# A two-layer decoder trunk on one core: the projection chunk with the sparse attention's keys and compressed input is put ahead of the chunk with its queries

## The chip, the cores and the metric

The kernel runs on one core of a Trainium2 chip. Its five instruction streams are TensorE (PE, with its weight loads as PEld), VectorE (DVE), ScalarE (ACT), GpSimd (POOL) and SyncE (SP, which here only issues DMAs). The metric is the time of one execution on the device, in microseconds (us).

## The reference

`x` is 256 tokens of 1024 numbers in float32. Each of two layers does this:

```python
x = x + 0.5 * swiglu_ffn(x, ffn1_norm[l], ffn1_wi[l], ffn1_wo[l])
h = rms_norm(x, mix_norm[l])
(sb_q, sb_k, sb_v, mla_cq, mla_ckv, mla_kr, nsa_q, ck, cv, sk, sv, wk, wv,
 nsa_gate, merge_gate) = jnp.split(h @ w_in[l], offsets, axis=-1)
o_sb  = stick_breaking_attention(sb_q, sb_k, sb_v)        # 8 heads of 64
o_mla = mla_attention(mla_cq, mla_ckv, mla_kr, ...)       # 8 heads, low rank
o_nsa = nsa_attention(nsa_q, ck, cv, sk, sv, wk, wv, nsa_gate, ...)
gates = jax.nn.sigmoid(merge_gate)
y = gates[0] * (o_sb @ proj_sb[l]) + gates[1] * (o_mla @ proj_mla[l]) \
  + gates[2] * (o_nsa @ proj_nsa[l])
x = x + y @ w_out[l]
x = x + 0.5 * swiglu_ffn(x, ffn2_norm[l], ffn2_wi[l], ffn2_wo[l])
```

In the sparse attention (NSA), `ck` and `cv` are the compressed input: windows of 32 tokens, 16 apart, get a position added and go through a two-layer network, which makes 15 compressed keys and values for each of two groups. `sk`, `wk` are the keys of its other two branches and `nsa_q` its queries; these are normalized and rotated.

## The kernel before, in words

The 256 tokens lie as two blocks `t` of 128. Every float32 operand is split into a high and a low half, and each product is three matmuls (`mm3`, L588 to L590: high by high, low by high, high by low, in the order in which the trace names them).

The mixer between the two feed-forward nets multiplies the normalized `h` with the input projection in chunks of 512 or fewer columns. The weights come in slabs of 256 rows. A slab is loaded on SP's queue, either as float32 (`raw`, L514, then split by ACT in L1042 and DVE in L1044) or from a copy that an earlier part of the program split already (`early`, L1030: four DMAs, two `whi` and two `wlo`). Four slab buffers go round. `t_chunk` (L1080) takes slab after slab: for each it issues 12 matmuls of 512 columns, six for each token block; a chunk of 1024 rows is 4 slabs and 48 matmuls. After a block's last matmul it starts the block's evacuation.

Which slab comes when is the list that `layer_plan` writes, and which chunk uses it is the order of the calls in `bulk()`; both have to agree. The two chunks of this case are

- the queries' chunk, columns 1952 to 2463 of `w_in`. Its evacuation `ev_nq` (L1393) is one ACT copy for each block into `nx` (L1395);
- the keys' chunk, 512 columns picked from 2464 on. Its evacuation `ev_nk` (L1398) copies the compressed input `ck`, `cv` into a scratch buffer `c2` (L1404, ACT), sends it by two SP DMAs for each block into the tile `zc`, in which two neighbouring tokens share a partition (L1406), and copies the keys into `nx` (L1412).

`zc` is read by `cmp_in` (L1804): four PE transposes (L1809) that wait for all four DMAs, DVE additions of the position (L1821), and a split into `zw` (L1068 on ACT, L1070 on DVE). `zw` is used much later, by the compression network. `nsa_prep` (L1761) normalizes and rotates queries and keys of a block together, so it needs both evacuations.

Beside `bulk()` other tasks of the mixer run: stick-breaking attention (`sb_head`, scores L1552 and L1558, ACT and DVE work on them, the reversal L1585 and L1586 on PE, `pv` with PV matmuls L1522 to L1528), and MLA, whose queries and keys are turned on DVE (`turn`, L1247), written to DRAM by POOL (L1249, `md`) and read back by POOL (L1257, `st`) in a layout for the scores. POOL also raises sums to a power for the norms (L595). MLA's softmax ends on ACT (L1668), and PE transposes its result (L1677).

All these tasks are generators. A `Planner` holds a clock for each of PE, ACT, DVE and POOL, with costs written in the program, asks each task for its next step, and gives the engine to the step that could start first, with small handicaps (`HOLDS`, `URGENCY`). The instructions of PE, DVE and ACT are written in the order of its choice. The queues of SP and POOL have their DMAs in the order in which the planner came to them, and an instruction that waits holds up those behind it. In the planner's clock a zc DMA lands 4.2 us after its copy:

```python
            z = Tok(k2.t + 4.2)
            s_wf.put(z)
            ev_zc[t].set(z)
```

Nothing measured goes back into it: the order is fixed when the program is built.

Of the kernel before, what the change touches and what calls it, by code (L numbers as in the profile page):

```python
# [16 lines left out]
D = 1024  # L17
# [5 lines left out]
KT = D // 128  # L23
# [9 lines left out]
def _k_slabs(rows, n, get, name="_fn"):  # L33

    kts = rows // 128
    g = min(kts, max(1, 1024 // n))
    out = []
    for k0 in range(0, kts, g):
        gg = min(g, kts - k0)

        def fn(inp, l, k0=k0, gg=gg):
            w = np.asarray(get(inp, l))[k0 * 128:(k0 + gg) * 128]
            return w.reshape(gg, 128, n).transpose(1, 0, 2).reshape(128, gg * n)

        fn.__name__ = name
        out.append((gg * n, fn))
    return out


def _cols(name, c0, n):  # L50
    return lambda inp, l: inp[name][l][:, c0:c0 + n]


def _cat(name, parts):
    return lambda inp, l: np.concatenate([np.asarray(inp[name][l][:, a:a + n]) for a, n in parts], 1)
# [7 lines left out]
def _w1(name, j0):  # L63
    def w1_slab(inp, l):
        w = np.asarray(inp[name][l]).reshape(16, 128, 128)[j0:j0 + 8]
        return w.transpose(1, 0, 2).reshape(128, 1024)
    return w1_slab


def layer_plan():  # L70

    plan = []

    def ffn(p):
        f0, fn = FFN_CHUNKS[0]
        plan.extend(_k_slabs(D, 2 * fn, _cat(p + "_wi", [(f0, fn), (DFF + f0, fn)])))
        for f0, fn in FFN_CHUNKS[1:]:
            for part in range(2):
                plan.extend(_k_slabs(D, fn, _cols(p + "_wi", part * DFF + f0, fn)))
        for kt in range(DFF // 128):  # L80
            plan.append((1024, lambda inp, l, kt=kt: inp[p + "_wo"][l][kt * 128:(kt + 1) * 128]))

    def merge(b, name):
        out = []
        for c in range(2):
            out.extend(_k_slabs(D, 512, _cols("w_in", 3256 + b * 1024 + c * 512, 512)))
            out.extend(_k_slabs(512, 512, _cols(name, c * 512, 512)))
        return out

    ffn("ffn1")  # L90
    plan.extend(_k_slabs(D, 440, _cat("w_in", [(1536, 416), (3232, 24)])))
    plan.extend(_k_slabs(D, 512, _cols("w_in", 0, 512)))
    plan.extend(_k_slabs(256, 768, lambda inp, l: inp["mla_w_uq"][l], "_uq"))
    sk = _k_slabs(D, 512, _cols("w_in", 512, 512))
    plan.extend(sk[:2])
    plan.append((1024, _ukv))
    plan.extend(sk[2:])
    plan.extend(_k_slabs(D, 512, _cols("w_in", 1024, 512)))
    plan.extend(_k_slabs(D, 512, _cols("w_in", 1952, 512)))
    plan.extend(_k_slabs(D, 512, _cat("w_in", [(2464, 128), (2592, 128), (2720, 128), (2976, 128)])))  # L100
    m = merge(0, "proj_sb")
    plan.extend(m[:4])
    plan.extend(_k_slabs(D, 256, _cat("w_in", [(2848, 128), (3104, 128)])))
    m = m[4:] + merge(1, "proj_mla")
    plan.extend(m[:W1K_AT])
    plan.extend((1024, _w1("cmp_wk1", j0)) for j0 in (0, 8))
    plan.extend(m[W1K_AT:W1V_AT])
    plan.extend((1024, _w1("cmp_wv1", j0)) for j0 in (0, 8))
    plan.extend(m[W1V_AT:])
    m = merge(2, "proj_nsa")  # L110
    plan.extend(m[0:4] + m[6:10] + m[4:6] + m[10:])
    for kt in range(KT):
        plan.append((1024, lambda inp, l, kt=kt: inp["w_out"][l][kt * 128:(kt + 1) * 128]))
    ffn("ffn2")
    return plan
# [127 lines left out]
class Planner:  # L243
# [11 lines left out]
    def spawn(self, gen, hold=0.0):  # L255
        try:
            self.live.append([hold, gen, next(gen)])
        except StopIteration:
            pass
# [68 lines left out]
def use_p(cols, count, *deps, slots=(), extra=0.0):  # L328

    o = count * max(cols / 2400.0 + 0.0135, 0.06) + extra  # L330
    return "P", o, o + 0.2, deps, slots
# [40 lines left out]
def decoder_trunk(ctx, tc, xt_in, wts, lcon, cst, out, depth=DEPTH):  # L372
    nc = tc.nc
    PSUM = bass.MemoryType.PSUM
    plan = layer_plan()
# [9 lines left out]
    def acc_tile():  # L385
        return pb.tile([128, 512], F, tag="ps", name="acc")
# [12 lines left out]
    def cut(pair, *ix):  # L399
        return pair[0][ix], pair[1][ix]  # L400
# [96 lines left out]
    def slab_at(i):  # L497
        l, j = stream[i]
        return l * LSZ + offs[j], plan[j][0], plan[j][1].__name__
# [86 lines left out]
    def mm3(o, a, b, start=False, stop=False, **kw):  # L586

        nc.tensor.matmul(o, a[0], b[0], start=start, stop=False, **kw)  # L588
        nc.tensor.matmul(o, a[0], b[1], start=False, stop=False, **kw)  # L589
        nc.tensor.matmul(o, a[1], b[0], start=False, stop=stop, **kw)  # L590
# [13 lines left out]
    def of_t(q):  # L604
        return [(q[0][:, :, t, :], q[1][:, :, t, :]) for t in range(NT)]
# [342 lines left out]
    def mixer(l):  # L948
        es = ExitStack()
        mp = es.enter_context(tc.tile_pool(name="mp", bufs=1))  # L950
        hT, sq = nxt[0]
        nxt_T = hT
        hT = of_t(hT)
# [55 lines left out]
        def take():  # L1009
            use_at[0] += 1  # L1010
            return use_at[0] - 1

        def mark():
            ev_used[used[0]].set(Tok(pl.clock["P"]))
            used[0] += 1
# [58 lines left out]
        def t_chunk(n, kts, lhs, evac, need=lambda t, k: ()):  # L1074
            g = min(kts, max(1, 1024 // n))
            ns = kts // g
            acc = [None] * NT
            for s in range(ns):
                while slab_at(use_at[0])[2] in side:
                    yield from side[slab_at(use_at[0])[2]]()  # L1080
                i = take()
                for t in range(NT):
                    for j in range(g):
                        k = s * g + j
                        e = slab_ev[i][0 if (j + 1) * n <= RAW else 1]
                        tok = yield use_p(n, 3, e, *need(t, k), slots=(s_acc,) if k == 0 else ())
                        if k == 0:
                            acc[t] = acc_tile()
                        sl = slabs[i][1]
                        mm3(acc[t][:, :n], cut(lhs[t], A, k, A), cut(sl, A, slice(j * n, (j + 1) * n)),  # L1090
                            start=k == 0, stop=k == kts - 1)
                    if s == ns - 1:
                        spawn(evac(t, acc[t], tok), 0.02)
                s_w.put(tok)
                mark()
# [68 lines left out]
        def lat():  # L1164

            js = [take() for _ in range(4)]
            a = [None] * NT
            for k in range(KT):
                i = js[k // 2]
                for t in range(NT):  # L1170
                    tok = yield use_p(440, 3, slab_ev[i][k % 2], ev_hT[k], slots=() if k else (s_acc,))
                    if not k:
                        a[t] = acc_tile()
                    mm3(a[t][:, :440], cut(hT[t], A, k, A), cut(slabs[i][1], A, slice((k % 2) * 440, (k % 2 + 1) * 440)),
                        start=k == 0, stop=k == KT - 1)
                    if k == KT - 1:
                        spawn(ev_lat(t, a[t], tok), 0.02)
                if k % 2:
                    s_w.put(tok)
                    mark()  # L1180
# [287 lines left out]
        def bulk():  # L1468
            yield from lat()
            yield from chunk_T(sb_qk(0, 0.125))  # L1470
            for t in range(NT):
                nc.sync.dma_start(xd[t], xs[t])
            yield from chunk_T(sb_qk(1, 1.0))
            yield from t_chunk(512, KT, hT, ev_v)
            yield from t_chunk(512, KT, hT, ev_nq)
            yield from t_chunk(512, KT, hT, ev_nk)
            yield from t_chunk(512, KT, hT, ev_gate_raw)
            yield from t_chunk(256, KT, hT, ev_rest)
            yield from merge(0, g0, ev_g0, o_sb, ev_osb, True)
            for b, (oT, ev_o) in enumerate(((o_sb, ev_osb), (o_mla, ev_omla))):  # L1480
                for c in range(2):
                    if b or c:
                        ths, ev = [None] * NT, events(NT)
                        yield from t_chunk(512, KT, hT, gate_ev(ths, ev))
                        yield from merge(c, ths, ev, oT, ev_o, b == 0)
                if b == 0:
                    ev_sbm.set(Tok(pl.clock["P"]))
            gs = [([None] * NT, events(NT)) for _ in range(2)]
            for c in range(2):
                yield from t_chunk(512, KT, hT, gate_ev(*gs[c]))  # L1490
            for c in range(2):
                yield from merge(c, *gs[c], o_nsa, ev_onsa, False, final=True)
# [715 lines left out]
```

## Time and profile before

| | us |
|---|---|
| median of 3 runs (lowest, highest) | 1247.59 (1246.65, 1249.44) |
| the profiled execution | 1247.43 |
| its span, first to last instruction | 1245.5 |
| PE busy in it | 1238.7 |
| DVE busy | 944.4 |
| ACT busy | 789.4 |
| POOL busy | 153.6 |
| granted PE clock | 1.000 |

How to read the lines: PE is TensorE's matmuls, PEld its weight loads, which overlap them. `L1809` is a line of the kernel, `tp<-ident,zc` the tiles written and read. A row of a timeline gives the start in us, the length, the engine, the line and the operation, its form, how many in a row (`x4`), and in brackets how long the engine stood idle before and what released it. Matmul lengths overlap one another, so the distance from start to start is what a matmul costs. `SPq` is SP's queue: the length there is that of the issue (or of a wait before the next), not of the transfer. Rows that end with `KB` and a number are DMA issues of a window: how many, the size of one, and the median us from issue to landing.

The queries' chunk ended near 252 us in layer 0 and 871 us in layer 1 (the first rows of L1395 at 252.33 and 871.30), the keys' chunk near 266 and 888 us (L1404 ran from 266.2 to 888.9).

### The profile page before, as it was taken

What the parts mean: (1) busy time and instruction counts of PE and PEld (TensorE: products, weight loads), DVE (VectorE), ACT (ScalarE), POOL (GpSimd) and SP (SyncE); (2) the same over time, 40 slices, a digit from 0 to 9 for tenths busy, and PEclk for the clock granted to TensorE, in tenths of its full rate; (3) what the DMA queues carried; (4) which work ended last, traced back from release to release, by engine and by line L of the source; (5) the groups of instructions that cost most, each with busy time, mean ns of one, the idle gap of its engine ahead of it and who ended that gap; (6) DMA issues with size and microseconds to landing.
All of it is one profiled execution on the core that took longest, in us unless ns stands there. A gap on an engine that the chain in (4) does not pass through costs nothing.

```text
span 1245.5 us, 26170 instructions
## 1 busy us (share of the span) xinstructions
PE 1238.7 (99%) x9318; PEld 1159.4 (93%) x9318; DVE 944.4 (76%) x1961; ACT 789.4 (63%) x1633; POOL 153.6 (12%) x247
## 2 busy tenths in 40 slices
PE   9999999999999999999999999999999999999998
PEld 9999999888878899999999999998888889999987
DVE  7876668988888777776578776689968987786644
ACT  6665557787887566565456565567767774565542
POOL 0011201232000001121001121013330000023000
PEclk9999999999999999999999999999999999999999
DMA  8899985677645568999768999666897555667653
GB/s 273 287 329 326 339 269 184 197 209 234 217 128 171 166 214 260 332 331 337 215 202 279 331 321 321 221 203 188 286 317 240 157 156 185 192 209 245 220 169 119
DMA packets 157122, 298.20 MB, mean 239 GB/s; under 512 B 21424, under 2 KB 24496, under 8 KB 156992
## 3 DMA queue, kind: packets, MB, share of 16 engines
q1 hardware_dynamic: 143872, 258.64, 64.9%
q0 software_dynamic: 13120, 37.89, 8.2%
q8 instruction: 73, 1.20, 0.4%
q14 instruction: 57, 0.47, 0.1%
HBM read 258.12 MB, written 37.81 MB: 238 GB/s over the span
## 4 chain that ended last, share of the span: by engine, by line
PE 94%; ACT 2%; DVE 2%; DMA 1%; issue 1%; POOL 0%; SPq 0%; DVEq 0%; ACTq 0%; POOLq 0%
PE acc L780 13%; PE acc L778 13%; PE acc L779 13%; PE acc L588 9%; PE acc L590 9%; PE acc L589 9%; PE acc L670 6%; PE acc L669 6%; PE acc L668 6%; PE acc L1204 1%; PE acc L1205 1%; PE acc L1206 1%; PE att L2041 1%; ACT wf L1636 1%; PE tp L2052 1%
## 5 line engine op out<-in xcount | busy, mean ns | idle before, releaser
L536 DVE TENSOR_TENSOR vlo<-raw,vhi 128x512 fp32r<-128x512 f32 x452 | 292.7, 685 | 90.9 <-ACT vhi L535 89.4
L535 ACT ACTIVATE vhi<-raw 128x512 fp32r<-128x512 f32 x452 | 263.5, 622 | 142.8 <-PE acc L779 43.1
L778 PE MATMUL acc<-hThi,vhi 128*128 128x256 f32 x1280 | 353.3, 276 | 0.0
L779 PE MATMUL acc<-hTlo,vhi 128*128 128x256 f32 x1280 | 353.3, 276 | 0.0
L780 PE MATMUL acc<-hThi,vlo 128*128 128x256 f32 x1280 | 353.3, 276 | 0.0
L780 PEld LDWEIGHTS acc<-hThi,vlo 128*128 128x128 f32 x1280 | 240.3, 188 | 0.0
L779 PEld LDWEIGHTS acc<-hTlo,vhi 128*128 128x128 f32 x1280 | 240.3, 188 | 0.0
L778 PEld LDWEIGHTS acc<-hThi,vhi 128*128 128x128 f32 x1280 | 240.3, 188 | 0.0
L1044 DVE TENSOR_TENSOR wlo<-raw,whi 128x512 fp32r<-128x512 f32 x216 | 141.2, 679 | 30.4 <-ACT whi L1042 28.6
L1042 ACT ACTIVATE whi<-raw 128x512 fp32r<-128x512 f32 x216 | 124.9, 616 | 47.8 <-PE acc L590 17.8
L670 PE MATMUL acc<-gh,vlo 128*128 128x256 f32 x528 | 145.7, 276 | 0.0
L668 PE MATMUL acc<-gh,vhi 128*128 128x256 f32 x528 | 145.7, 276 | 0.0
L669 PE MATMUL acc<-gl,vhi 128*128 128x256 f32 x528 | 145.7, 276 | 0.0
L588 PE MATMUL acc<-whi,hThi 128*128 128x512 f32 (+2 forms) x352 | 138.1, 392 | 0.0
L590 PE MATMUL acc<-whi,hTlo 128*128 128x512 f32 (+2 forms) x352 | 133.4, 379 | 0.0
L589 PE MATMUL acc<-wlo,hThi 128*128 128x512 f32 (+2 forms) x352 | 133.4, 379 | 0.0
L536 DVE TENSOR_TENSOR wlo<-raw,whi 128x512 fp32r<-128x512 f32 (+2 forms) x109 | 69.9, 677 | 45.4 <-ACT whi L535 45.1
L535 ACT ACTIVATE whi<-raw 128x512 fp32r<-128x512 f32 (+2 forms) x109 | 63.2, 617 | 57.7 <-PE acc L590 26.4
L554 ACT ACTIVATE ehi<-eraw 128x512 fp32r<-128x512 f32 x60 | 38.0, 633 | 97.3 <-DMA eraw<-in_wts 95.7
L669 PEld LDWEIGHTS acc<-gl,vhi 128*128 128x128 f32 x528 | 99.1, 188 | 0.0
L670 PEld LDWEIGHTS acc<-gh,vlo 128*128 128x128 f32 x528 | 99.1, 188 | 0.0
L668 PEld LDWEIGHTS acc<-gh,vhi 128*128 128x128 f32 x528 | 99.1, 188 | 0.0
(350 smaller groups left out, 2502.1 us busy)
## 6 DMA issues: line engine op xcount, KB each, us to landing
raw<-in_wts SPq DMA_DIRECT2D x764, 256.0 KB, 3.6
eraw<-in_wts SPq DMA_DIRECT2D x60, 256.0 KB, 5.2
early<-ehi POOLq DMA_DIRECT2D x60, 256.0 KB, 4.3
early<-elo POOLq DMA_DIRECT2D x60, 256.0 KB, 4.6
whi<-early SPq DMA_DIRECT2D x60, 256.0 KB, 4.2
wlo<-early SPq DMA_DIRECT2D x60, 256.0 KB, 4.5
st<-md POOLq DMA_DIRECT2D x33, 64.0 KB, 4.4
xd<-x SPq DMA_DIRECT2D x4, 512.0 KB, 2.6
```

Of the source, the lines that this page charges most:

```text
L535: nc.scalar.activation(hi[:, q], raw[:, o:o + g], AF.Copy)
L536: last_lo[0] = nc.vector.tensor_tensor(lo[:, q], raw[:, o:o + g], hi[:, q], op=OP.subtract).ins
L588: nc.tensor.matmul(o, a[0], b[0], start=start, stop=False, **kw)
L589: nc.tensor.matmul(o, a[0], b[1], start=False, stop=False, **kw)
L590: nc.tensor.matmul(o, a[1], b[0], start=False, stop=stop, **kw)
L668: nc.tensor.matmul(o, sl[0][:, w], h, start=k == 0 and c == 0, stop=False)
L669: nc.tensor.matmul(o, sl[0][:, w], l_, start=False, stop=False)
L670: nc.tensor.matmul(o, sl[1][:, w], h, start=False, stop=k == kts - 1 and c == 1)
L778: nc.tensor.matmul(o, sl[0][:, w], h, start=k == 0 and c == 0, stop=False)
L779: nc.tensor.matmul(o, sl[0][:, w], l_, start=False, stop=False)
L780: nc.tensor.matmul(o, sl[1][:, w], h, start=False, stop=k == KT - 1 and c == 1)
L1044: nc.vector.tensor_tensor(hl[1][:, c:c + m], raw[:, :m], hl[0][:, c:c + m], op=OP.subtract)
```

## The change

Two lines trade places in `layer_plan`, and the two calls in `bulk()`.

```diff
--- before.py
+++ after.py
@@ -96,8 +96,8 @@
     plan.append((1024, _ukv))
     plan.extend(sk[2:])
     plan.extend(_k_slabs(D, 512, _cols("w_in", 1024, 512)))
+    plan.extend(_k_slabs(D, 512, _cat("w_in", [(2464, 128), (2592, 128), (2720, 128), (2976, 128)])))
     plan.extend(_k_slabs(D, 512, _cols("w_in", 1952, 512)))
-    plan.extend(_k_slabs(D, 512, _cat("w_in", [(2464, 128), (2592, 128), (2720, 128), (2976, 128)])))
     m = merge(0, "proj_sb")
     plan.extend(m[:4])
     plan.extend(_k_slabs(D, 256, _cat("w_in", [(2848, 128), (3104, 128)])))
@@ -1472,8 +1472,8 @@
                 nc.sync.dma_start(xd[t], xs[t])
             yield from chunk_T(sb_qk(1, 1.0))
             yield from t_chunk(512, KT, hT, ev_v)
+            yield from t_chunk(512, KT, hT, ev_nk)
             yield from t_chunk(512, KT, hT, ev_nq)
-            yield from t_chunk(512, KT, hT, ev_nk)
             yield from t_chunk(512, KT, hT, ev_gate_raw)
             yield from t_chunk(256, KT, hT, ev_rest)
             yield from merge(0, g0, ev_g0, o_sb, ev_osb, True)
```

The planner then writes another order. Three places show it.

PE, layer 1, where the transposes of `zc` (L1809) stand now. The rows L1522 to L1528 are PV matmuls of stick-breaking pairs, L588 to L590 the matmuls of a slab.

```order
L1522 MATMUL acc<-wr,V_11466 128x256
L1524 MATMUL acc<-wr,V_11466 128x128
L1527 MATMUL acc<-wr,V_11466 64x128
L1528 MATMUL acc<-wr,V_11466 64x256
L588 MATMUL acc<-whi,hThi 128x512
L589 MATMUL acc<-wlo,hThi 128x512
L590 MATMUL acc<-whi,hTlo 128x512
L1809 MATMUL tp<-ident,zc 128x128 x4
L1522 MATMUL acc<-wr,V_11466 128x256
L1524 MATMUL acc<-wr,V_11466 128x128
```

They stand between the PV of the first pair and that of the second, three slab matmuls behind the first; before, they stood 77 rows further on, behind the scores of the third pair. Ahead of this place six slab matmuls less are left than before. Layer 0 shows the same rows here, and there they stood 58 rows further on. Behind the second PV come twelve slab matmuls and then a reversal (L1585).

SP, layer 0: before, then now. L514 is a raw load, L1030 the load of a slab split early, L1406 the DMAs into `zc`.

```order
L514 DMA raw<-in_wts 128x512 x38
L1030 DMA whi<-early 128x512
L1030 DMA wlo<-early 128x512
L1030 DMA whi<-early 128x512
L1030 DMA wlo<-early 128x512
L514 DMA raw<-in_wts 128x512 x2
L1030 DMA wlo<-early 128x512
L1030 DMA whi<-early 128x512 x2
L1030 DMA wlo<-early 128x512
L514 DMA raw<-in_wts 128x512
L1406 DMA zc<-wf 64x4x64 x2
L514 DMA raw<-in_wts 128x512
```

```order
L514 DMA raw<-in_wts 128x512 x37
L1406 DMA zc<-wf 64x4x64 x2
L514 DMA raw<-in_wts 128x512
L1030 DMA whi<-early 128x512
L1030 DMA wlo<-early 128x512
L1030 DMA whi<-early 128x512
L1030 DMA wlo<-early 128x512
L1406 DMA zc<-wf 64x4x64 x2
L514 DMA raw<-in_wts 128x512 x2
```

The first block's two DMAs now stand ahead of a slab's four loads, the second block's two right behind them. In layer 1 the four zc DMAs stood together, behind two raw loads and twelve L1030 loads; now it reads

```order
L1406 DMA zc<-wf 64x4x64 x2
L1030 DMA whi<-early 128x512
L1030 DMA wlo<-early 128x512
L1030 DMA whi<-early 128x512
L1030 DMA wlo<-early 128x512
L1406 DMA zc<-wf 64x4x64 x2
L514 DMA raw<-in_wts 128x512 x2
```

so that the first two stand ahead of one slab's loads, the last two behind it, and two raw loads that stood ahead come after them.

On ACT the copies of the compressed input (L1404) stand where those of the queries (L1395) stood; the second one of layer 0 has two splits (L1042), three casts (L1060) and one L1590 ahead of it since the first. On DVE the additions (L1821) move up into the stick-breaking stage with their splits, and in layer 0 the last turning of the MLA keys (L1247) moves from row 266 to row 306. So POOL's queue is different there, before and now (`rs` is the power, `md` and `st` are the turned queries and keys on the way to DRAM and back):

```order
L1249 DMA md<-mk 768x1x32 x8
L595 TENSOR_TENSOR rs<-ss,mh 128x12
L1257 DMA st<-md 32x2x256 x9
L595 TENSOR_TENSOR rs<-ss,mh 128x12
L1257 DMA st<-md 32x2x256 x3
```

```order
L1249 DMA md<-mk 768x1x32 x4
L595 TENSOR_TENSOR rs<-ss,mh 128x12
L1249 DMA md<-mk 768x1x32 x4
L595 TENSOR_TENSOR rs<-ss,mh 128x12
L1257 DMA st<-md 32x2x256 x12
```

All twelve reads now stand behind the second power. The number of instructions of PE, ACT and DVE for this work does not change.

## The prediction

> **What bounds the kernel now.** I read the page's head, granted clock and chain first.
>
> ```profile
> span 1245.5 us, 26170 instructions
> PE 1238.7 (99%) x9318; PEld 1159.4 (93%) x9318; DVE 944.4 (76%) x1961; ACT 789.4 (63%) x1633; POOL 153.6 (12%) x247
> ...
> PEclk9999999999999999999999999999999999999999
> ...
> PE 94%; ACT 2%; DVE 2%; DMA 1%; issue 1%; POOL 0%; SPq 0%; DVEq 0%; ACTq 0%; POOLq 0%
> ```
>
> PE is busy for 99% of the span at full clock and is 94% of the chain. A change that neither adds nor removes a matmul can act only through what PE waits for. That is the waits view of PE (total, times, longest):
>
> ```profile
> PE acc L421 <- DVE warm L418: 1.5, 1, 1.5
> PE tp L1809 <- DMA zc<-wf: 0.5, 1, 0.5
> PE tp L1950 <- DVE wf L1945: 0.3, 1, 0.3
> ...
> PE tp L1677 <- ACT wf L1668: 0.2, 1, 0.2
> ```
>
> Beside the start there is about 1 us in all, half of it in front of the four transposes of the compressed input (L1809). So there is little to gain, and the change moves just that place. Its timeline in layer 0, then the view of tile zc for both layers:
>
> ```profile
> 272.49 0.39 PE L590 MATMUL acc<-whi,hTlo 128*128 128x512 f32 x1
> 273.42 0.63 PE L1809 MATMUL tp<-ident,zc 128*128 128x128 f32 x4 [0.54 <-DMA zc<-wf]
> ```
>
> ```profile
> L1406 SPq DMA_DIRECT2D zc<-wf x8: 594/604/698, 267.2 to 890.1; - x8
> ...
> DMA to landing us min/median/max: 2.1/3.7/5.0
> ```
>
> A 512-column matmul starts every 0.23 us (rows below), so L1809 could have started at 272.72 and waited **0.7 us** start to start. In layer 1 the waits view has no such wait. A zc DMA occupies SP for 0.6 us and lands 2.1 to 5.0 us after its issue.
>
> **The change part by part.** *Matmuls, evictions, splits.* The two chunks have the same 48 matmuls each, and L1395, L1404 and L1412 run as often as before: nothing, by the same counts. What moves is time of arrival. By the program orders, PE meets L1809 after fewer matmuls: right behind the first stick-breaking PV and three matmuls. Six 512-column matmuls (6 x 0.23 = 1.37 us) are gone ahead of that place in both layers.
>
> *Layer 0.* Where PE will ask, and what the DMAs wait for:
>
> ```profile
> 261.18 0.39 PE L588 MATMUL acc<-whi,hThi 128*128 128x512 f32 x1
> 261.42 0.39 PE L589 MATMUL acc<-wlo,hThi 128*128 128x512 f32 x1
> ```
>
> ```profile
> 253.27 0.68 ACT L1395 ACTIVATE nx<-acc,rn 128x512 f32<-128x512 f32 x1
> 253.84 1.15 ACT L1042 ACTIVATE whi<-raw 128x512 fp32r<-128x512 f32 x2
> 254.88 1.35 ACT L1060 ACTIVATE wr<-wf 128x384 fp32r<-128x384 f32 x3
> ```
>
> The first PV ends at 261.18, now 261.18 - 1.37 = 259.81, and with three matmuls PE asks at 260.5. On ACT the second L1404 now stands behind these two splits, three casts and one L1590: it begins near 256.3 and, at 0.46 us, ends near 256.75. SP issues the last two zc DMAs then, at about 256.9 and 257.6, right behind four loads of prepared slabs (L1030). Fastest landing 257.6 + 2.1 = 259.7, no wait. The same DMAs behind a load took 4.1 in this layer:
>
> ```profile
> zc<-wf SPq DMA_DIRECT2D x4, 64.0 KB, 4.1
> ```
>
> That makes 261.0 for the first, 261.7 for the second: a wait of 0.5 to 1.2. I take 0.9, towards the latter, because loads are ahead in the queue. Instead of 0.7 it is **+0.2** (bounds -0.7 and +0.5).
>
> *Layer 1.* PE's side, SP's side, and the landings of two short windows there:
>
> ```profile
> 871.52 0.39 PE L588 MATMUL acc<-whi,hThi 128*128 128x512 f32 x1
> ...
> 878.07 0.28 PE L1522 MATMUL acc<-wr,V 128*128 128x256 f32 x1
> ...
> 878.78 0.39 PE L588 MATMUL acc<-whi,hThi 128*128 128x512 f32 x1
> ```
>
> ```profile
> 873.55 0.33 SPq L1030 DMA_DIRECT2D wlo<-early  x1
> 873.98 0.97 SPq L1030 DMA_DIRECT2D whi<-early  x2
> 875.04 5.40 SPq L1030 DMA_DIRECT2D wlo<-early  x2
> ...
> 887.08 1.27 SPq L1406 DMA_DIRECT2D zc<-wf  x2
> ```
>
> ```profile
> wlo<-early SPq DMA_DIRECT2D x2, 256.0 KB, 4.6
> ```
>
> ```profile
> zc<-wf SPq DMA_DIRECT2D x4, 64.0 KB, 2.8
> ```
>
> PE asks at 878.78 - 1.37 + 0.69 = 878.1. Before, the four zc DMAs stood at 887, far behind these loads. Now two stand ahead of a slab's four loads and two directly behind them. The loads cannot go earlier: their buffer is freed by nine matmuls after 871.52, at 873.6, and the first row starts there. Four issues last to about 875.7 (873.55, 873.98 twice, 875.04). So the last two zc DMAs go at about 875.7 and 876.5, though ACT has their copy near 874:
>
> ```profile
> 871.30 0.67 ACT L1395 ACTIVATE nx<-acc,rn 128x512 f32<-128x512 f32 x1
> ...
> 872.81 1.35 ACT L1060 ACTIVATE wr<-wf 128x384 fp32r<-128x384 f32 x3
> ```
>
> Bounds: 876.5 + 2.1 = 878.6, a wait of 0.5; with layer 0's 4.1, 880.6, a wait of 2.5. The load ahead, issued at 875.2, takes 4.6 and lands at 879.8; zc came behind its predecessors in both layers, so 880.4 is nearest: **+2.3**, where there was none.
>
> Behind L1809 on PE stand the second PV and twelve slab matmuls, which all move by the wait. On DVE, the additions on the transposed input (L1821) stand ahead of an L1580 which the next reversal (L1585) needs. The rows of these two kinds:
>
> ```profile
> 282.09 0.72 DVE L1821 TENSOR_TENSOR tmp<-tp,lc 128x240 f32<-128x240 f32 x2
> ```
>
> ```profile
> 882.99 0.55 DVE L1580 TENSOR_TENSOR wr<-wf,wr 128x384 fp32r<-128x384 f32 x1
> ```
>
> The transposes start at 880.4 and end near 881.1; four additions take 1.4, a copy and L1580 (0.55 for each) make 883.6. PE reaches L1585 after the transposes (0.4 from row to row), the second PV (0.7, as the first from 878.07 to 878.78) and twelve matmuls of 0.23, at 884.2. Covered by 0.6; without that, what is late is late on PE one to one. The two raw loads that stood ahead of the slab come at 877; five more us and two splits make 884.5, ahead of their chunk near 888 (the last L1404 now stands at 888.9).
>
> *What it moves on POOL.* In layer 0 the second token block's turned MLA keys (L1247) move back on DVE past the earlier additions, and all st reads stand behind POOL's second 12-wide power (L595).
>
> ```profile
> 260.39 0.97 DVE L1247 STREAM_TRANSPOSE mk<-mk 128x768 f32<-128x768 f32 x1
> ...
> 290.20 0.17 DVE L594 TENSOR_SCALAR ss<-ss 128x12 f32<-128x12 f32 x1
> ```
>
> ```profile
> 271.71 1.66 POOL L1257 DMA_DIRECT2D st<-md  x3
> ...
> 290.52 2.30 POOL L595 TENSOR_TENSOR rs<-ss,mh 128x12 f32<-128x12 f32 x1 [2.72 <-DVE ss L594]
> ```
>
> ```profile
> st<-md POOLq DMA_DIRECT2D x3, 64.0 KB, 2.9
> ```
>
> ```profile
> 287.81 0.62 ACT L1068 ACTIVATE qk<-st 96x512 fp32r<-96x512 f32 x1
> ```
>
> ```profile
> 297.29 0.22 PE L588 MATMUL att<-qk 96*128 96x128 f32 x1
> ```
>
> L594 is the 310th DVE row in both programs, so at the latest near 290.2, and near 287.5 if DVE gains the 2.5 us of L1821 and splits now done earlier. Then power 2.3, three issues 1.7, landing 2.9, two splits 1.3: 295.7 to 298.5. The scores of the first MLA pair move from 297.29 to 298.7 and, with layer 0's +0.2, to 298.9. Hidden, with 0.4 to 3 us of cover: **0**.
>
> *Later waits.* DVE is free earlier around 282 to 290, which can take away the 0.3 at L1950; some softmaxes lie about 1.2 us closer to their transposes (L1677), which already wait now. Bounds -1 and +0.7; I take **-0.3**.
>
> Sum: +0.2 + 2.3 + 0 - 0.3 = **+2.2**. The profiled execution took 1247.43, of which 1245.5 is span; with +2.2 it is **1249.6**. The median of the runs, 1247.59, is 0.16 above the profiled one, less than the runs differ.
>
> The Trainium skill, "DMA: Bandwidth & Descriptors", section "Anatomy of one DMA — SWDGE (gpsimd) path", gives a fixed 2.0 us and bytes at 436 GB/s for a DMA that GpSimd issues. As an estimate from that page 64 KB take 2.15 us, and layer 1 would wait 0.5 instead of 2.3, with 1247.0 for the sum. The fastest zc DMA (2.1) agrees; the medians 2.8 and 4.1 do not.
>
> **The rivals.** *(B) The compressed input is there early.* zc lands 2.1 us after issue in spite of the load ahead. Layer 0 loses its 0.7, layer 1 waits 0.5, later waits -0.3: 1247.43 - 0.7 + 0.5 - 0.3 = 1246.9. For it: the minimum of 2.1, and a small DMA among large ones. Against: medians of 2.8 and 4.1 where the queue was loaded. The page's estimate above is this rival.
>
> *(C) Slower: the turned MLA keys are late.* If L594 falls two us later than before, at 292.2, because L1247 and the reductions it moved among wait for something I took as ready, the chain ends at 300.5, and PE waits 1.6 in front of the first MLA scores, on top of the forecast: 1251.2; up to 1252.5 with the +0.7 of the softmaxes. It decides from L594 at 290.6 on. For it: POOL is in order and every st read is now behind that one power. Against: DVE has less to do just before it.
>
> *(D) A gain.* Both zc waits vanish (-0.7), and the softmax transposes gain from a DVE that is free earlier. Their source view has this:
>
> ```profile
>   ACT wf L1668: 3.4, 11
> ```
>
> Half of it would be -1.7, the 0.3 at L1950 added: 1244.7. Against: most of the 3.4 are weight loads behind which PE still works.
>
> *(E) The clock falls.* Should the layer 1 wait grow beyond my bound, PE could come out of it slower, as at the start:
>
> ```profile
> 1.46 3.36 PE L421 MATMUL acc<-warm 128*128 128x512 f32 x7 [1.46 <-DVE warm L418]
> ```
>
> Seven 512-column matmuls take 3.36 there, 0.48 each where 0.23 is usual: half rate. Four us of it would cost 2, with a wait of 3.5 in all 0.2 + 3.5 + 2 - 0.3 = +5.4: 1252.8. No wait before was longer than 1.5. The Trainium skill, "TensorE: Matmul & The Clock Gate", section "What's actually happening", sets the fall at about 3.4 us of idling; no run here shows it, and my 2.3 stays below it.
>
> That the change does not do what it says: the compressed input is earlier, but its consumers in the compression come tens of us later at unchanged places, so nothing is won by that; this is in all cases.
>
> **How the numbers follow.** Forecast 0.48 (own range 1248.4 to 1250.8), B 0.24, C 0.18, D 0.06, E 0.04. A measurement of this kernel tells a difference from 0.2% on, 2.5 us: 1245.1 and 1250.1. Faster is D: 0.06. Slower is C and E but for 0.01, and the upper 0.18 of the forecast: 0.39. The rest, 0.55, is the same. The range reaches from below B's 1246.9 to C's upper part: 1246.6 to 1252.2; outside are D, E and the ends of B and C.
>
> **What would show it.** Right: L1809 in layer 1 waits 1.8 to 2.8 for zc, and in layer 0 about 0.9; zc's last DMAs issue at about 876 and land directly behind the slab. Wrong: landings within 2.5 us there (B); a wait in front of the first MLA scores in layer 0 (C); a granted clock below 1 near 880 (E); the PE waits for L1668 gone (D). Any wait over 1 us at a place not named makes the sum wrong.

## The result, and the profile after

| | before | changed |
|---|---|---|
| median, us | 1247.55 (6 runs) | 1254.94 (6 runs, 1252.55 to 1255.45) |
| ratio | 1 | 1.0057 (95% interval 1.0046 to 1.0068) |
| span of the profiled execution | 1245.5 | 1253.3 |
| mean granted clock in it | 1.000 | 0.997 |

The change makes the kernel 7.4 us slower. The forecast was 1249.6 with a range up to 1252.2, so both the size and the range were wrong. The page's head of the changed kernel, to be read beside that of before:

```profile
span 1253.3 us, 26167 instructions
PE 1241.2 (99%) x9318; PEld 1161.0 (93%) x9318; DVE 945.6 (75%) x1969; ACT 787.0 (63%) x1625; POOL 153.3 (12%) x247
...
PEclk9999999999999999999999999999899999999999
...
PE 91%; ACT 3%; DMA 2%; DVE 2%; issue 1%; SPq 0%; POOL 0%; DVEq 0%; ACTq 0%
```

PE has the same 9318 matmuls; one of its 40 clock digits is an 8. The waits of PE (total, times, longest):

```profile
PE tp L1809 <- DMA raw<-in_wts: 4.4, 2, 3.8
PE acc L421 <- DVE warm L418: 1.5, 1, 1.5
PE tp L1677 <- ACT wf L1668: 0.9, 2, 0.5
PE acc L851 <- ACT whi L535: 0.6, 1, 0.6
PE tp L1876 <- DVE wf L1872: 0.5, 1, 0.5
```

The transposes of zc wait 4.4 us where they waited 0.5. The releaser named is a raw load, but it cannot be one in layer 1: the two raw loads behind zc (issued at 880.83 and 881.48, 3.5 us each) landed at 884.36 and 884.97, after the transposes had begun. What the transposes read is zc, whose last DMA landed at 883.84. The place in layer 1 on PE's timeline, and the granted clock (third column from the end) in windows of 2 us, which also list the busy time of PE, PEld, DVE, ACT and POOL:

```profile
879.88 0.40 PE L590 MATMUL acc<-whi,hTlo 128*128 128x512 f32 x1
884.04 1.08 PE L1809 MATMUL tp<-ident,zc 128*128 128x128 f32 x4 [3.76 <-DMA raw<-in_wts]
...
886.20 0.63 PE L588 MATMUL acc<-whi,hThi 128*128 128x512 f32 x1
886.63 0.63 PE L589 MATMUL acc<-wlo,hThi 128*128 128x512 f32 x1
```

```profile
879.00:881.00 2.00, 1.27 (x10) 0.80 (x8) 0.00 (x0) 0.80 (x2) 0.00 (x0) 1.00 1.02 338
881.00:883.00 2.00, 0.00 (x0) 0.00 (x0) 1.72 (x4) 1.98 (x6) 0.00 (x0) 0.91 0.96 260
883.00:885.00 2.00, 0.96 (x5) 0.99 (x6) 1.42 (x3) 1.97 (x5) 0.00 (x0) 0.50 0.46 173
885.00:887.00 2.00, 2.00 (x11) 1.86 (x11) 1.80 (x6) 0.77 (x3) 0.00 (x0) 0.50 0.00 0
887.00:889.00 2.00, 2.00 (x6) 1.56 (x5) 1.97 (x4) 1.85 (x5) 0.00 (x0) 0.50 0.00 0
```

PE could have gone on at 880.11 and starts at 884.04: 3.93 us. Then it runs at half clock until about 889.5: the last two 512-column matmuls above start 0.43 apart instead of 0.23. From 884.04 to 889.5 that is some 2.7 us of work lost.

**Where the 7.8 us of span lie.** Outside the mixers both kernels have the same matmuls in the same order, and inside them the orders meet again at several places, where the same matmuls have been done in both. There the start of the matmul with the same number (counted from 0) can be compared (worked out from PE's timelines):

| matmul number | before | changed | difference |
|---|---|---|---|
| 215, first feed-forward net | 30.05 | 30.62 | +0.57 |
| 2002, ahead of the moved chunks, layer 0 | 250.14 | 250.71 | +0.57 |
| 2277, ahead of the first MLA scores | 297.06 | 297.14 | +0.07 |
| 2303, behind the first of them | 301.20 | 301.58 | +0.38 |
| 2893, end of layer 0's mixer | 400.07 | 402.06 | +1.98 |
| 6795, ahead of the moved chunks, layer 1 | 870.02 | 872.03 | +2.01 |
| 7127, layer 1's MLA | 925.00 | 932.78 | +7.77 |
| 9301, near the end | 1240.04 | 1247.80 | +7.76 |

The first 0.57 comes with the wait for the first weight split (L851), which lies ahead of everything the change touches. Layer 0 costs 1.4, layer 1 costs 5.75: 3.9 of wait, 2.7 of clock, less 0.9 that comes back between 895 and 925.

### The profile page after: what moved, and what is told of

It reads as the page before. It is cut to its first block, busy times and chain, and to the rows that moved or that the text cites. A ratio compares the mean times of both kernels' runs of the same rounds, so it can differ in the third digit from the quotient of the medians.

```text
span 1253.3 us, 26167 instructions
## 1 busy us (share of the span) xinstructions
PE 1241.2 (99%) x9318; PEld 1161.0 (93%) x9318; DVE 945.6 (75%) x1969; ACT 787.0 (63%) x1625; POOL 153.3 (12%) x247
## 4 chain that ended last, share of the span: by engine, by line
PE 91%; ACT 3%; DMA 2%; DVE 2%; issue 1%; SPq 0%; POOL 0%; DVEq 0%; ACTq 0%
PE acc L778 12%; PE acc L779 12%; PE acc L780 12%; PE acc L588 9%; PE acc L589 8%; PE acc L590 8%; PE acc L669 6%; PE acc L670 6%; PE acc L668 6%; PE acc L1204 1%; PE acc L1205 1%; PE acc L1206 1%; DMA raw<-in_wts 1%; PE att L2041 1%; ACT wf L1636 1%; PE tp L2052 1%
## 5 line engine op out<-in xcount | busy, mean ns | idle before, releaser
L1042 ACT ACTIVATE whi<-raw 128x512 fp32r<-128x512 f32 x216 | 124.9, 616 | 46.0 <-PE acc L590 17.2
L588 PE MATMUL acc<-whi,hThi 128*128 128x512 f32 (+2 forms) x352 | 137.9, 392 | 0.0
L590 PE MATMUL acc<-whi,hTlo 128*128 128x512 f32 (+2 forms) x352 | 133.9, 381 | 0.0
L555 DVE TENSOR_TENSOR elo<-eraw,ehi 128x512 fp32r<-128x512 f32 x60 | 41.4, 691 | 80.4 <-ACT ehi L554 80.2
```

## The experiments

The theory after the result: zc lands late in layer 1, because it stands behind a slab's loads in a queue whose DMA engines are full, and PE's idling then makes the clock fall; these two are nearly all of the loss. Rivals: the loss is spread over both layers; POOL's reads are what slows the loads; the clock falls for another reason. All times of before are those measured beside the run on the same chip. "Loss" is the difference of matmul starts as in the table, layer 0 from number 2002 to 3072 (behind its mixer), layer 1 from 6740 (behind 860) to 7637 (1010).

### One layer at a time

```diff
-            yield from t_chunk(512, KT, hT, ev_nk)
-            yield from t_chunk(512, KT, hT, ev_nq)
+            for ev in (ev_nk, ev_nq) if l == 1 else (ev_nq, ev_nk):
+                yield from t_chunk(512, KT, hT, ev)
```

(an excerpt; the slabs of the other layer are back in their old order, and for layer 0 alone the test is `l == 0`)

> The two chunks trade places in layer 1 only, in slabs and program; layer 0 is as before. Theory (nearly all of the loss is layer 1's wait for zc and the half clock behind it): L1809 in layer 1 waits 3 to 4 us, the granted clock falls behind it, and the time is 5 to 7 us above before, 1252.5 to 1254.5. Rival (the loss is spread over both layers, by softmaxes that lie closer to their transposes): at most 4 us above before.

> The two chunks trade places in layer 0 only. Theory: L1809 in layer 0 waits 0.8 us as it did, some softmax waits of layer 0 grow, 0 to 2 us above before, 1247.5 to 1249.5, clock 1.000 throughout. Rival (spread over both layers): 3 us or more above before.

Layer 1 alone: 1251.86, before 1247.3, ratio 1.0040 (1.0025 to 1.0055). Its profiled execution took 1255.06, with a wait of 4.7 us at L1809, a half clock behind it and a loss of 6.8 in layer 1; the other three runs took 1251.7 to 1252.0. Layer 0 alone: 1250.22, ratio 1.0027 (1.0017 to 1.0037), clock 1.000 in seven of eight runs, loss 2.6 in layer 0 and none in layer 1. The two add up to the whole (+4.6 and +2.9). Layer 1 has the larger part, as the theory has it, but its +4.6 is short of the 5 to 7 that the theory gave and above the rival's 4, and layer 0's share is above the theory's 0 to 2 and just short of the rival's 3. The theory was half right.

### The clock

```diff
             tp = tp_tile()
+            for _ in range(14 if l else 0):
+                nc.tensor.matmul(tp, rt[:, 0:128], rt[:, 0:512], start=True, stop=True)
             for i in range(4):
                 nc.tensor.transpose(tp[:, i * 128:(i + 1) * 128], zc[0]...
```

> The changed kernel with 14 matmuls of 512 columns on constants put ahead of the four transposes in layer 1; their result is overwritten by the transposes. They keep PE busy for 3.2 of the 3.9 us of the wait, and the transposes still start when zc lands. Theory (PE's own idling made the clock fall): granted clock 1.0 from 883 to 890, the half-rate matmuls are gone, about 2.9 us less than the changed kernel, near 1252. Rival (the clock falls for something else, as load on the chip): clock still about 0.5 there, and no gain.

1254.0, before 1247.3, ratio 1.0051 (1.0036 to 1.0066). PE's timeline and the clock of this run:

```profile
881.22 3.38 PE L1809 MATMUL tp<-rt 128*128 128x512 f32 x14
884.93 0.63 PE L1811 MATMUL tp<-ident,zc 128*128 128x128 f32 x4 [0.33 <-DMA zc<-wf]
```

```profile
883.00:885.00 2.00, 1.67 (x9) 1.07 (x8) 1.97 (x5) 1.98 (x6) 0.00 (x0) 1.00 0.97 297
885.00:887.00 2.00, 2.00 (x16) 1.86 (x17) 1.99 (x7) 1.97 (x6) 0.00 (x0) 1.00 0.05 20
```

The transposes begin 3.7 us after PE was free, as late as in the changed kernel, but the clock stays at 1.00, there and in all four runs. Layer 1 loses 3.0 instead of 5.75: the clock's price is 2.8 us in these two profiles. The whole is only 0.3 to 0.9 us below the changed kernel's two medians (1254.27 and 1254.94), not 2.9: layer 0 lost 3.5 in this run instead of 1.4, and several runs of the changed kernel had no half clock in the first place (one of six, and two of four when it was repeated). So it is shown that PE's idling makes the clock fall, and the mean price of that is below that of the profiled run. The ten runs of the changed kernel say the same without any edit: the three at clock 1.000 took 1252.55 to 1253.76 us, the seven others 1254.62 to 1257.09.

With 6 matmuls instead of 14:

> As the run with 14 matmuls ahead of the transposes in layer 1, but with 6 of them (1.4 us), so that PE idles for about 2.5 us instead of 3.9. Theory (the clock falls after a few us of idling of PE, not from the wait's mere presence): with 2.5 us of idling the clock stays at 1.000 in most runs; time as with 14 matmuls, 1252.5 to 1254.5. Rival (any such wait makes it fall): mean clock 0.997 to 0.999 in most runs, and the half-rate matmuls behind the wait are back.

1254.22, before 1247.59, ratio 1.0043 (1.0028 to 1.0058). Three of five runs had clock 1.000, and the time lies in the range that the theory gave. The profiled run was not one of the three, with only 2.5 us of idling:

```profile
884.59 0.63 PE L1811 MATMUL tp<-ident,zc 128*128 128x128 f32 x4 [2.33 <-DMA zc<-wf]
```

```profile
883.00:885.00 2.00, 0.41 (x5) 0.44 (x5) 1.97 (x5) 1.94 (x6) 0.00 (x0) 1.00 0.77 258
885.00:887.00 2.00, 2.00 (x13) 1.80 (x12) 1.86 (x6) 1.58 (x4) 0.00 (x0) 0.58 0.01 2
```

The clock falls at 885.3, when PE has been busy again for 0.7 us. Neither text foresaw that; the last section takes it up.

### Why zc lands late

The landings of the changed kernel, by DMA views of single issues: SP's rows first, then for the issue at 877.48 (the slab's fourth load, which is the row `wlo`), and for the last zc pair.

```profile
872.45 0.33 SPq L1030 DMA_DIRECT2D whi<-early  x1
...
874.57 1.27 SPq L1406 DMA_DIRECT2D zc<-wf  x2
875.94 0.55 SPq L1030 DMA_DIRECT2D whi<-early  x1
...
877.48 0.44 SPq L1030 DMA_DIRECT2D wlo<-early  x1
878.91 1.82 SPq L1406 DMA_DIRECT2D zc<-wf  x2
```

```profile
wlo<-early SPq DMA_DIRECT2D x1, 256.0 KB, 6.0
```

```profile
zc<-wf SPq DMA_DIRECT2D x2, 64.0 KB, 4.4
```

877.48 + 6.0 = 883.5 for the slab, and zc 0.2 and 0.4 behind it, at 883.65 and 883.84. It took 11.4 us from the first load of the slab before (872.45). POOL's first three st reads had moved into this stretch (873 to 875), which the forecast did not look at, and the third and fourth load of the slab before landed 5.5 and 5.9 us after their issue instead of 4.3 and 4.8. That was the next suspect.

```diff
-... (*ev, gate(MLA_AT, p, -4)), (s_th,)
+... (*ev, *((ev_mk[0],) if l and p == 0 and i == 0 else ()), gate(MLA_AT, p, -4)), (s_th,)
```

> The changed kernel, but in layer 1 POOL's first three st reads wait for the first token block's turned MLA keys, so that they stand behind those four md writes as before. Theory (these reads share the DMA engines with the slab ahead of zc, whose third and fourth loads land 5.5 and 5.9 us after their issue instead of 4.3 and 4.8, and so hold back SP's next DMAs): slab loads land about 1.1 us earlier, the last zc DMAs are issued 1.1 earlier, the wait at L1809 is 2.5 to 3.0, and the clock stays at 1.0: 3 to 4 us less than the changed kernel, 1251 to 1252. Rival (the loads are slow for another reason): wait of 3.9 as in the changed kernel, same time within 1 us.

1255.32, before 1247.3, ratio 1.0061 (1.0044 to 1.0078): no gain. The slab before did land sooner (4.8 and 5.0 us after issue), and the last zc pair was issued 5.7 us after its first load instead of 6.5, as expected. But zc landed at the same distance from that load, 11.35 us, again directly behind the slab's fourth load:

```profile
873.29 0.33 SPq L1030 DMA_DIRECT2D whi<-early  x1
...
878.96 1.27 SPq L1406 DMA_DIRECT2D zc<-wf  x2
```

```profile
zc<-wf SPq DMA_DIRECT2D x2, 64.0 KB, 5.2
```

An earlier issue only waits longer. The wait was 3.9, as the rival said. In this run no read of POOL's is issued between 868 and 890, so the reads are not the cause. In five other profiles with the loads of the changed kernel the distance from the first load of the slab before to zc's last landing is 11.2 to 12.2 us.

The next run takes zc out of SP's queue.

```diff
-                nc.sync.dma_start(zc[0]...
+                nc.scalar.dma_start(zc[0]...
```

> The changed kernel with the eight zc DMAs issued on ACT's queue instead of SP's. PE's order is the same. Theory (zc lands late because it stands behind a slab's loads in SP's queue): the last zc DMAs of layer 1 are issued near 876.5 and land 2 to 4 us later, wait at L1809 0 to 1.5, clock 1.000, 1249 to 1251.5. Rival (the DMA engines are full, whatever the queue): they land with the slab near 883, wait 3 us or more, half clock behind it, 1253 or more.

1259.26, before 1247.24, ratio 1.0087 (1.0072 to 1.0102). The first zc pair, issued by ACT at 876.73 and 877.37, took 7.4 us and landed with the slabs' loads, which the rival expected. In the waits view L1809 has only 0.4 left, but a larger wait stands where ACT is late:

```profile
zc<-wf ACTq DMA_DIRECT2D x2, 64.0 KB, 7.4
```

```profile
PE acc L1522 <- ACT nx L1412: 4.3, 1, 4.3
```

```profile
884.63 0.47 ACT L1404 ACTIVATE wf<-acc,rn 128x256 f32<-128x256 f32 x1 [4.49 <-DMA zc<-wf]
```

ACT's second copy now waits until the first pair has landed, which it did not in the changed kernel (there it ran at 875.70, and the first pair landed at 880). Why this edit makes it wait was not found, and the wait is a cost of the edit, so only the first pair's landing counts here. It says that the place in SP's queue alone does not decide; the DMA engines are full in this stretch (the share of 0.96 to 1.02 in the windows of the changed kernel from 879 to 883). The following run then takes bytes away: in layer 1 the slab ahead of the last zc pair is loaded as float32 (two loads of 256 KB) instead of as two halves (four).

```diff
         for a in EARLY_AT[part]:
+            if l and a == 27:
+                continue
```

> The changed kernel, but in layer 1 the slab whose loads stand directly ahead of the last zc DMAs is no longer split early: it is loaded as float32, two loads of 256 KB instead of four, and split by ACT and DVE. Theory (the DMA engines move what stands ahead of zc in the ring at about 250 GB/s, whatever the issue times): half a MB less is 2 us, the last zc DMA lands 8.7 to 9.7 us after the first load of the slab before (11.4 in the changed kernel), the wait at L1809 is 1.5 to 2.5, the clock stays at 1.000, 1250 to 1252. Rival (latency of single DMAs or late issues set it): landing still 11 us after that load, wait 3.5 or more, 1254 or more.

```profile
876.95 0.33 SPq L1032 DMA_DIRECT2D whi<-early  x1
...
881.54 1.26 SPq L1408 DMA_DIRECT2D zc<-wf  x2
```

```profile
zc<-wf SPq DMA_DIRECT2D x2, 64.0 KB, 4.7
```

```profile
884.37 0.40 PE L592 MATMUL acc<-whi,hTlo 128*128 128x512 f32 x1
886.75 0.52 PE L1811 MATMUL tp<-ident,zc 128*128 128x128 f32 x3 [1.98 <-ACT wf L1568]
```

The last zc DMA lands at 886.6, 9.65 us after the first load instead of 11.4, and below the 11.2 to 12.2 of the profiles with the full loads; the wait is 2.15, the clock stays at 1.00 there, and layer 1 loses 2.9. All of that is as the theory gave it. The total, 1256.37 against 1247.59, ratio 1.0053 (1.0033 to 1.0073), with 1252 to 1257 from run to run, is not: layer 0 lost 5.6 in the profiled run, 3.1 of it around the first MLA scores, where the clock fell too, and 0.8 came between the mixers. The edit shows that zc's landing is set by the loads ahead of it. It takes away two loads along with their bytes, so whether the bytes or the number of loads decide is not shown; and it is no remedy.

### Moving the transposes back

```diff
-            ev_zc[t].set(z)
+            ev_zc[t].set(Tok(k2.t + 9.0))
```

> The changed kernel, in which the planner is told that zc lands 9.0 us after its copy instead of 4.2, so that it puts L1809 behind more matmuls. Theory (only the place of L1809 against zc's landing is wrong): no wait over 0.3 us at L1809 in either layer, clock 1.000 everywhere, 1247 to 1249.5; what is left above before are softmax waits in layer 0. Rival (the earlier keys and compressed input cost elsewhere too, on DVE and ACT): 1250.5 or more.

1259.42, before 1247.24, ratio 1.0087 (1.0071 to 1.0104). No wait at L1809 is left, and the kernel is slower still:

```profile
PE att L588 <- ACT qk L1068: 3.1, 1, 3.1
```

This wait is in front of the first MLA scores of layer 0, and the clock falls there (at 300.47). The additions and splits of zw ran at 266.5 to 270.6 and are not in its way. The st reads are issued at 294.9, 0.6 us after the last of POOL's md writes landed (294.28); the last two writes took 6.2 us, with six loads of SP issued around them (286.9 to 289.5). It is rival C's place. Layer 0 loses 6.5 and layer 1 still 3.2. The theory "only the place of L1809 is wrong" falls.

The same small edit (5.2 us) on the kernel before:

> The kernel before, in which the planner is told 5.2 us instead of 4.2 for zc. Theory: the wait at L1809 in layer 0 (0.7 in the profile of before) shrinks below 0.2 and nothing else moves: 0.5 to 0.8 us less than before, 1246.5 to 1247. Rival: other waits take its place, no gain.

1248.42, before 1247.24, ratio 1.0008 (0.9998 to 1.0017): the wait in layer 0 is gone from the waits view, but a wait of 0.75 came up at L1677 in layer 1. No gain, as the rival said.

### The softmaxes of layer 0

In the seven profiles of the new order in layer 0 without a half clock there, the stretch from number 2303 to the end of the mixer loses 1.6 us. (The 1.4 in the expectation below is counted from number 2323, where the orders have not yet met.) In the changed kernel PE's waits there are 0.9 us longer than before in all, at L1677, L1876 and L2020.

```diff
-                k = yield "P", 0.53, 0.73, ev_E[i], ...
+                k = yield "P", 0.53, 0.73, [Late(e, 0.5 if l == 0 else 0.0) for e in ev_E[i]], ...
```

(`Late` is the same time with 0.5 added)

> The changed kernel, in which the planner takes the softmax results of layer 0 to be 0.5 us later than it did when it places their transposes (L1677), so that more matmuls stand ahead of them. Between the first MLA scores and the end of layer 0's mixer the changed kernel loses 1.4 us in every profile taken so far. Theory (the new order puts these transposes closer behind their scores than ACT and DVE can follow): waits at L1677 and L1876 in layer 0 shrink from 2.5 to under 1, that stretch loses at most 0.5, and the time is about 1 us less than the changed kernel, 1252.5 to 1254.5. Rival (DVE and ACT have more to do there, wherever the transposes stand): the waits move to the next matmuls and the stretch loses 1.2 or more.

1257.67, before 1247.84, ratio 1.0067 (1.0045 to 1.0090). The waits at L1677 went, and others came, in the softmax's neighbours:

```profile
PE att L601 <- DVE qk L1082: 1.1, 3, 0.4
PE att L600 <- ACT qk L1080: 1.1, 1, 1.1
```

The stretch lost 3.2 instead of 1.6, part of it by a half clock from 344.6 to 348.0. The theory that the transposes stand too close to their scores is refuted as a sufficient cause; which work on DVE and ACT makes the 1.6 us was not found and stays open.

The same on the kernel before, in both layers with 0.4:

> The kernel before, in which the planner takes the softmax results of both layers to be 0.4 us later for their transposes (L1677). In its profile PE waits there 2.2 us in layer 0 and 2.2 in layer 1. Theory: half to all of it goes, 1 to 3 us less than before, 1244.5 to 1246.5, which would beat both kernels. Rival: the matmuls put ahead are missing elsewhere, 1247 to 1248.5.

1246.61, before 1247.84, ratio 0.9992 (0.9982 to 1.0002), between what theory and rival gave. Its profile has 1.1 less in layer 0 and 0.7 less in layer 1, but in time it can't be told from before. No version was found that clearly beats it.

### The changed kernel once more

> The changed kernel itself once more, beside the next three. Both theories: 1253 to 1256, wait at L1809 in layer 1 of 3.5 to 4.7 us, the last zc DMA lands within 0.5 us behind the slab's fourth load.

1254.27, before 1247.24, ratio 1.0051 (1.0032 to 1.0070); wait at L1809 4.5 us, the last zc DMA 0.4 us behind the slab's fourth load, loss 1.8 and 5.3. Two of its four runs had clock 1.000, and these were the two fastest (1252.67 and 1253.76).

## Why the prediction was wrong

**The bound and the place were right.** PE sets the time, the count of matmuls is unchanged, and the largest new wait is L1809 in layer 1 on zc. PE asked at 880.1; the forecast's 878.1, with the 2.0 that the whole had slipped by then, is the same.

**The step that failed** is this one: "The load ahead, issued at 875.2, takes 4.6 and lands at 879.8". The 4.6 was the median of two different issues. The row of that issue alone, in the profile of before:

```profile
wlo<-early SPq DMA_DIRECT2D x1, 256.0 KB, 6.4
```

With 6.4 the load lands at 881.4 (as its trace in before has it), zc at about 881.8, and the wait is 3.7 instead of 2.3. Measured: 3.9. The forecast also capped the wait at 2.5 by letting zc take 4.1 us from its own issue; the run with later st reads shows that its issue does not matter, since it lands directly behind what stands ahead. Two raw loads (0.5 MB) left the stretch, but a zc pair and three st reads (0.3 MB) came in; from the first load of the slab before to the slab's fourth it took 11.0 us as before, and zc another 0.4.

**The clock.** Because the wait was bounded at 2.5, the rival E ("the clock falls") got a chance of 0.04. It is what happened in most runs. Its price stood there as "Four us of it would cost 2"; in the profile it was 5.5 us of work at half rate and 2.7 lost. Its total, 1252.8, is 2.3 below the profiled execution (1255.11); 1.5 of that is layer 0, and 0.6 is there ahead of the change. The Trainium skill, "TensorE: Matmul & The Clock Gate", section "What's actually happening", has a rule that speaks against the change; it was read there as a threshold of 3.4 us on the wait, and the runs do not bear that reading out (below).

**Layer 0.** "+0.2" for L1809 fits this profile, where the wait is 0.77 for a forecast of 0.9. Seven other profiles of this order have 1.1 to 2.1 there, three of the old order 0.4 to 1.6; up to the first MLA scores six profiles of the new order lie at -0.5 to +0.8 against before, so it is within scatter. "Hidden, with 0.4 to 3 us of cover: **0**" failed, and by a step that its sum does not have. The sum goes from L594 over the power to the reads. But a read needs the turned keys in DRAM, so it also waits until POOL's md writes have landed, and these start only after the moved L1247 (at 284.17):

```profile
285.44 2.88 POOL L1249 DMA_DIRECT2D md<-mk  x4 [11.95 <-DVE mk L1247]
288.25 2.38 POOL L595 TENSOR_TENSOR rs<-ss,mh 128x12 f32<-128x12 f32 x1
291.55 1.66 POOL L1257 DMA_DIRECT2D st<-md  x3 [0.91 <-ACT V L1231]
```

```profile
md<-mk POOLq DMA_DIRECT2D x1, 96.0 KB, 3.4
```

```profile
st<-md POOLq DMA_DIRECT2D x3, 64.0 KB, 5.2
```

```profile
299.13 0.33 PE L589 MATMUL att<-qk 96*128 96x128 f32 x1 [0.17 <-DVE qk L1070]
```

L594 ran at 287.55 (forecast 287.5). The power began 0.5 us after its end, when POOL had issued its writes, and ended at 290.63, 0.8 later than the sum has it. The last write, issued at 287.55, landed at 290.94, and the first read went out at 291.55, 0.9 after the power. The row names ACT's L1231 as the releaser, but in all ten profiles of the new order in layer 0 the first read follows the last write's landing by 0.6 us, while it follows the power's end by 0.4 to 3.6. Then the three reads took 5.2 us instead of 2.9 (the median), from first issue to last landing 6.0 instead of 4.6. These three parts, 0.8, 0.9 and 1.4, make the 3.1 us that used up the cover: 0.3 us were lost between the numbers 2277 and 2303, and 0.3 to 1.6 in the six other profiles of this order without a half clock there. The 5.2 was to be seen: the reads issued at 286.21 in the profile of before took 4.6 to 5.1. So rival C had the right place and the right name, the turned keys are late; its path, a late L594, was not the one. "I take **-0.3**" for the later waits has the wrong sign: layer 0 lost 1.6 between 301 and 400; layer 1 gained 0.9 after 895. The upper price of C, 1252.5, does not come out of its terms either: 1251.2 with +0.7 in place of -0.3 is 1252.2.

**Rival B** (zc lands 2.1 us after its issue) fell: 4.1 to 4.7 for the last pair in the changed kernel, 7.4 on ACT's queue. The Trainium skill, "DMA: Bandwidth & Descriptors", section "Anatomy of one DMA — SWDGE (gpsimd) path", gave 2.15 as an estimate by its fixed cost. That agrees with the fastest zc DMA of this trace (2.1, issued at 254.20 behind one raw load and the first of its pair), not with this stretch. **Rival D** did not occur.

**The chances.** 0.39 for slower was too little, and the range's upper end of 1252.2 left out E, whose condition was not as remote as the mis-sized wait made it.

## What to carry to other kernels

When a small DMA is moved ahead, take its landing from what stands ahead of it in the stretch where it will stand: add up the bytes, or take the landing of the very load ahead, issue by issue. A median over two issues can hide a factor of two (6.4 and 2.75 us here), and issuing the small DMA earlier, or on another queue, gained nothing here while the engines were full. When work moves whose result goes out to DRAM and is read back, put the landing of the write into the sum. Price a long wait of PE with the clock as well: here 3.9 us of wait cost up to 2.8 more, and 2.5 us were enough to make the clock fall.

## What the runs showed of the hardware

The half clock comes in pieces of one length, and at times that do not follow the wait. In windows of 0.2 us the changed kernel's clock falls at 882.65 and comes back at 889.48:

```profile
882.60:882.80 0.20, 0.00 (x0) 0.00 (x0) 0.20 (x2) 0.20 (x1) 0.00 (x0) 0.63 0.81 307
...
889.40:889.60 0.20, 0.20 (x2) 0.16 (x2) 0.20 (x1) 0.00 (x0) 0.00 (x0) 0.80 0.00 0
```

That is 6.83 us. Worked out in the same way, the other falls inside the mixers lasted 6.8 or 3.4 us, nothing between. After PE had gone idle in layer 1 the clock fell 2.5 us later (changed kernel) to 5.0 us later (the repeat), in the latter and with 6 matmuls ahead only when PE was at work again.

What orders them is a grid of steps of 3.413 us, half the length of that fall, which lies differently in each execution. At the start of the changed kernel the 256-column matmuls of L851 to L853 stand 0.21 us apart up to 5.25 and 0.12 from 5.45, and its trace has the first full clock at 5.43. From there to the fall are 257 steps, and 2 more to the return. In the eight other profiles, too, each fall and each return lies a whole number of these steps behind the first rise, to 0.01 us; over all fourteen profiles the first rise lies between 4.56 and 7.41 us. The share of PE's busy time in the step that ends with the fall, and in the one behind it:

| profile, fall at (us) | step before | step behind | half clock, us |
|---|---|---|---|
| changed kernel, 882.65 | 30% | 59% | 6.8 |
| layer 1 alone, 882.79 | 0% | 73% | 6.8 |
| zc on ACT, 885.85 | 6% | 67% | 6.8 |
| transposes moved back, 300.47 | 37% | 64% | 6.8 |
| st later, 884.38 | 4% | 86% | 3.4 |
| the repeat, 885.20 | 14% | 100% | 3.4 |
| 6 matmuls ahead, 885.32 | 32% | 100% | 3.4 |
| softmax transposes later, 887.34 | 9% | 87% | 3.4 |
| softmax transposes later, 344.62 | 63% | 100% | 3.4 |
| raw slab, 302.97 | 68% | 100% | 3.4 |

Over all fourteen profiles the clock fell behind each of the eleven steps with 40% or less (three of them in the last microseconds of a run) and behind none of the thirteen with 45 to 62% at full clock. It came back after one step where PE was busy for 86% or more of the step behind the fall, and after two where it was 59 to 73%. The last two rows do not fit: in the raw slab's, PE had two waits of 0.7 and 0.4 us in front of the first MLA scores, and other steps with 63 to 73% brought no fall. What sets these two apart stays open.

The grid agrees with what the Trainium skill, "TensorE: Matmul & The Clock Gate", says in the section "What's actually happening", that activity is watched in free-running windows of about 3.4 us. But idling for a whole window was not needed: 2.5 us of idling were enough in the run with 6 matmuls, where they lay within one step, while the 2.15 us at 884.6 in the run with the raw slab left 45% of a step busy and did not make the clock fall. So a wait of 2.5 to 4 us has a price that changes from run to run, by how much of it falls into one step.
